# Which operand stands still in the expert value products: coefficients or value rows

## The chip, the cores and the metric

The kernel runs on one core of one Trainium2 chip. The metric is the device time of one execution in microseconds (us). PE is TensorE (PEld its weight loads), DVE is VectorE, ACT is ScalarE, POOL is GpSimd, SP is SyncE, which here only issues DMA.

## The reference, cut to what matters

The program is one attention block with a mixture of experts behind it (`first_block`), and a second block with attention, a state space branch and a gated feed-forward layer (`second_block`), on 256 tokens of 2048 features in fp32. The change touches one sum of the first block, the last line of the expert layer:

```python
idx = jnp.take_along_axis(cand_i, best_j, axis=-1)      # 16 experts of 16384 for each token and head
g = jax.nn.softmax(best_s, axis=-1)
u_sel = jnp.take(u, idx, axis=0)
a = jax.nn.gelu(jnp.einsum('thkd,td->thk', u_sel, hb), approximate=False)
v_sel = jnp.take(v, idx, axis=0)
return jnp.einsum('thk,thkd->td', (g * a).astype(hb.dtype), v_sel)
```

`u` and `v` are 16384 x 2048 tables. The kernel gathers nothing: it computes gelu(u x) for all 16384 experts and 256 tokens, multiplies it by a dense table of the weights g (zero where an expert was not chosen), and multiplies the result, the coefficients, by all of `v`.

## The kernel before, in words

The activations lie as columns: `xT[k]` is a tile of 128 features by 256 tokens, k = 0 to 15. Every fp32 product is made of three matmuls in a faster format: each operand is split into a high and a low part (ACT rounds the high part, DVE subtracts it from the source for the low part), and `mm3` (lines 177 to 182) issues high x high, high x low and low x high into the same PSUM sums. The first argument of `mm3` is the stationary operand (loaded into the array before each matmul, the PEld rows), the second the moving one.

The expert layer works in 128 blocks of 128 experts. For each block `scores` (989) makes 48 matmuls with rows of `u` as the stationary operand and 256 tokens moving, and a gelu. 30 blocks later `coef` (1050) multiplies by the weights and splits the result into `ahi` and `alo` (128 experts x 256 tokens, in the first two blocks a tile named `first`). The value products are cut into 256 half steps: `place(n)` gives the half of the features (1024 of 2048) and the block. Eight blocks of one half follow each other, then the same eight blocks of the other half. For a half step `v_split` (1009) loads two blocks of `v` at a time into a `raw` tile (five such tiles rotate among all loads of the program) and splits 128 experts x 1024 features into `wp` or `vp` tiles, and `v_main` (1085) makes the products: for each 128 of the 1024 features the value rows are the stationary operand and the coefficients of 256 tokens move. That is 8 x 3 = 24 matmuls in a half step. The sums of the first four of the eight feature tiles stay in PSUM (`ps_v`, two banks for a half) through all 128 blocks; those of the other four lie in two `ps_t` banks and are added to `xT` by DVE after each group of eight blocks (`add`, 1109, line 1112).

The order on every engine is the order of the Python code; nothing is rescheduled. The expert loop has three stretches. `FILL` (1141): six half steps alone. The loop (1145): two half steps with 24 score matmuls after each. The end (1157): the remaining half steps without scores, where `v_split` and `ahead` run three steps ahead, and where the parameters of the state space branch and the modulation sums (`self.more`) are worked in. The last half step but one and the last are made together (1174). Behind them comes the norm of the next block: `sq_add` (347) squares each finished `xT` tile on ACT and adds the squares on POOL or DVE, and `make` (394) sums them on PE.

Of the kernel before, what the change touches and what calls it, by code (L numbers as in the profile page):

```python
# [14 lines left out]
OP = mybir.AluOpType  # L15
# [3 lines left out]
KT = D // 128  # L19
T = 256  # L20
# [16 lines left out]
class Pipe:  # L37
# [73 lines left out]
    def add(self, gen):  # L111
        self.side.append(gen)


class Core:
# [11 lines left out]
    def sb(self, pool, name, shape, dt=F32, bufs=1, tag=None):  # L127
        return pool.tile(list(shape), dt, name=name, tag=tag or name, bufs=bufs)
# [337 lines left out]
    def mixer(self, pool, upto):  # L466
        nc, ins, sb = self.nc, self.ins, self.sb
        mm = nc.tensor.matmul
        w_in, w_out = ins["w_in"][0], ins["w_out"][0]
        x, meta = ins["x"][0], ins["meta_tokens"]  # L470
# [16 lines left out]
        rows = [(xa[0], 128), (xa[1], 128), (xm, 16)]  # L487
# [38 lines left out]
            nc.vector.tensor_tensor(self.both, self.ident[:40, 0:8], self.ident[:40, 32:40], op=OP.add)  # L526


        self.xT = [sb(self.glob, "xT", [128, T], bufs=KT) for _ in range(KT)]
        self.gap(self.glob, "hh", 32)  # L530
        hh = sb(self.glob, "hh", [128, KT, N], F32R)
        hl = sb(self.glob, "hl", [128, KT, N], F32R)
# [2 lines left out]
        turned = []  # L535
# [375 lines left out]
    def peer(self, ctx, pool, upto):  # L911
        nc, ins, sb = self.nc, self.ins, self.sb
        mm = nc.tensor.matmul
        u, v = ins["peer_u"][0], ins["peer_v"][0]
        BI, WI = 8, 4
# [48 lines left out]
        turned = []  # L964
# [35 lines left out]
        vt, vs, spare = {}, {}, {}  # L1000
# [4 lines left out]
        def place(n):  # L1005
            b, r = divmod(n, 2 * BI)
            return r // BI, b * BI + r % BI
# [40 lines left out]
        coefs = {}  # L1048

        def coef(i):  # L1050
            if i % WI == 0 and i:
                weights(i // WI + 1)
            a = act.pop(i)
            w = wb[i // WI][:, :, i % WI, :]
            nc.vector.tensor_tensor(a.rearrange("p (c t) -> p c t", c=16), a.rearrange("p (c t) -> p c t", c=16), w, op=OP.mult)  # L1055
            if i < 2:
                hi, lo = (sb(wp, "first", [128, T], F32R, bufs=4) for _ in range(2))
                if i == 1:
                    self.gap(wp, "first", 160)
            else:  # L1060
                if i == 2:
                    self.gap(spare["v"], "ahi", 192)
                hi, lo = (sb(spare["v"], nm, [128, T], F32R, bufs=10) for nm in ("ahi", "alo"))
            nc.scalar.activation(hi, a, AF.Copy)  # L1064
            coefs[i] = (hi, lo)
            return lambda: nc.vector.tensor_tensor(lo, a, hi.bitcast(F32), op=OP.subtract)

        def ahead(n):

            if n < 256:  # L1070
                half, i = place(n)
                if half == 0:
                    return coef(i)
            return nothing
# [5 lines left out]
        with self.tc.tile_pool(name="experts", bufs=1) as ep:  # L1080
            banks = {}
            spare["v"] = ep
            self.gap(ep, "vp", 64)

            def v_main(*ns):


                half, i = place(ns[0])
                end = place(ns[-1])[1]
                if i == 0:  # L1090
                    banks[half] = [self.ps("v") for _ in range(2)]
                if i % BI == 0:
                    banks["t"] = [self.ps("t") for _ in range(2)]

                def at(d):
                    return (banks[half] if d < 4 else banks["t"])[d // 2 % 2][:, (d % 2) * T:(d % 2 + 1) * T]

                for d in range(8):
                    first, last = (i == 0, end == 127) if d < 4 else (i % BI == 0, end % BI == BI - 1)
                    c = slice(d * 128, (d + 1) * 128)  # L1100
                    for n in ns:
                        hi, lo = vs[n]
                        self.mm3(at(d), (hi[:, c], lo[:, c]), coefs[place(n)[1]], first and d % 2 == 0, last and n == ns[-1], skip_group_check=True)
                for n in ns:
                    vs.pop(n)
                    if half == 1:
                        coefs.pop(place(n)[1])

                def add():
                    for d in range(0 if end == 127 else 4, 8):  # L1110
                        x = self.xT[half * 8 + d]
                        nc.vector.tensor_tensor(x, at(d), x, op=OP.add)
                        if end == 127:
                            self.sq_add(half * 8 + d, x)

                return add if end % BI == BI - 1 else nothing

            reorder()
            self.spare = "g"
            n = 0  # L1120

            def half_step(n, block=None, half=0, ticks=0):

                def more(i):
                    if i < ticks:
                        next(self.more, None)

                add = v_main(n)
                low = v_split(n + 1)
                if block:  # L1130
                    block[0](half)
                low()
                more(0)
                if block:
                    block[1](half)
                add()
                low = ahead(n + 2)
                more(1)
                low()

            while n < FILL:
                half_step(n)
                n += 1
            new = blocks(LAG + 1)
            for i in range(LAG, 128):
# [947 lines left out]
```

## Time and profile before

| what | value |
|---|---|
| median of 3 runs (lowest, highest) | 3706.91 us (3699.51, 3732.38) |
| the profiled execution | 3723.51 us |
| its span | 3721.7 us |
| mean granted TensorE clock | 0.99 of full speed |
| PE busy, PEld busy | 98%, 95% of the span |
| DVE, ACT, POOL busy | 76%, 49%, 13% of the span |

The profile is of one execution, and 16.6 us above the median. Matmuls are pipelined and each row lasts until its modelled end, so consecutive rows overlap: how fast PE works is read from the starts of consecutive rows, or from the count of matmuls in a stretch, not from the duration of one row.

### The profile page before, as it was taken

How to read it: one execution, taken by the hardware profiler on the slowest of the kernel's cores; microseconds unless marked ns; L12 is line 12 of the kernel's file. 1: busy time of each engine (PE TensorE's matmuls, PEld its weight loads, DVE VectorE, ACT ScalarE, POOL GpSimd, SP SyncE). 2: the span in 40 equal slices, each digit the busy share in tenths (PEclk: the TensorE clock that was granted, in tenths of full speed). 3: DMA queues.
4: the chain of work that ended last, by engine and by line, in shares of the span. 5: the costliest groups of instructions: out<-in, count | busy, mean ns of one | idle time of the engine just before them, and what ended most of it. 6: DMA issues, size and time to landing. Idle time of an engine off the chain costs nothing.

```text
span 3721.7 us, 72639 instructions
## 1 busy us (share of the span) xinstructions
PE 3629.0 (98%) x30186; PEld 3536.0 (95%) x30186; DVE 2831.7 (76%) x4414; ACT 1819.5 (49%) x2740; POOL 479.7 (13%) x496
## 2 busy tenths in 40 slices
PE   9999999999999999999999999898999999999998
PEld 8989899999899999999999998888889999999998
DVE  5556678988688888888888779999888675656565
ACT  4444444369444444444444456665544554444443
POOL 0000012100000000000000015666520100000000
PEclk9999999999999999999999999999999999999999
DMA  6546464455998999999999756545477675556563
GB/s 207 170 136 204 159 193 151 170 170 201 278 252 245 245 250 254 249 257 251 253 250 255 259 193 200 173 158 175 155 225 240 202 238 190 182 182 196 175 196 125
DMA packets 491481, 768.99 MB, mean 207 GB/s; under 512 B 21050, under 2 KB 332501, under 8 KB 485248
## 3 DMA queue, kind: packets, MB, share of 16 engines
q1 hardware_dynamic: 476160, 712.11, 62.8%
q0 software_dynamic: 14960, 52.23, 5.0%
q8 instruction: 237, 3.88, 0.4%
q14 instruction: 92, 0.75, 0.1%
q10 hardware_dynamic: 32, 0.01, 0.0%
HBM read 734.92 MB, written 27.26 MB: 205 GB/s over the span
## 4 chain that ended last, share of the span: by engine, by line
PE 79%; DVE 10%; ACT 6%; issue 3%; DMA 2%; POOL 0%; SPq 0%; DVEq 0%; POOLq 0%; ACTq 0%
PE ps_g L180 18%; PE ps_g L181 18%; PE ps_g L182 18%; DVE wp L149 4%; PE ps_v L181 3%; PE ps_v L182 3%; PE ps_v L180 3%; PE ps_t L181 3%; PE ps_t L182 3%; PE ps_t L180 3%; DMA raw<-in_peer_u_dram 1%; ACT wp L148 1%; PE ps_t L942 1%; ACT raw L1379 1%; PE ps_v L1377 1%
## 5 line engine op out<-in xcount | busy, mean ns | idle before, releaser
L180 PE MATMUL ps_g<-hh,wp 128*128 128x256 f32 (+1 forms) x5648 | 1608.8, 285 | 0.4 <-ACT wp L148 0.3
L182 PE MATMUL ps_g<-hh,wp 128*128 128x256 f32 (+1 forms) x5648 | 1585.3, 281 | 12.6 <-DVE wp L149 12.6
L181 PE MATMUL ps_g<-hl,wp 128*128 128x256 f32 (+1 forms) x5648 | 1584.1, 280 | 2.8 <-DVE hl L1628 2.8
L149 DVE TENSOR_TENSOR wp<-raw,wp 128x1024 fp32r<-128x1024 f32 (+2 forms) x877 | 1055.3, 1224 | 67.8 <-ACT wp L148 66.8
L180 PEld LDWEIGHTS ps_g<-hh,wp 128*128 128x128 f32 x5648 | 1069.4, 189 | 24.8 <-issue 16.8
L182 PEld LDWEIGHTS ps_g<-hh,wp 128*128 128x128 f32 x5648 | 1070.6, 190 | 16.8 <-DVE wp L149 16.2
L181 PEld LDWEIGHTS ps_g<-hl,wp 128*128 128x128 f32 x5648 | 1072.2, 190 | 3.6 <-DVE hl L1628 3.0
L148 ACT ACTIVATE wp<-raw 128x1024 fp32r<-128x1024 f32 (+2 forms) x877 | 869.8, 1014 | 403.8 <-PE ps_g L181 206.0
L979 DVE STREAM_TRANSPOSE raw<-raw 128x1024 f32<-128x1024 f32 x196 | 242.7, 1239 | 58.0 <-DMA raw<-in_peer_u_dram 56.5
L870 DVE SCALAR_TENSOR_TENSOR macc<-raw,cs,macc 128x512 f32<-128x512 f32 x360 | 283.2, 787 | 3.9 <-DMA raw<-in_w_mod_dram 3.9
L1023 DVE TENSOR_TENSOR wp<-raw,wp 128x1024 fp32r<-128x1024 f32 x155 | 186.5, 1206 | 39.0 <-ACT wp L1021 38.7
L1021 ACT ACTIVATE wp<-raw 128x1024 fp32r<-128x1024 f32 x155 | 163.0, 1055 | 99.2 <-PE ps_t L181 45.0
L180 PE MATMUL ps_g<-act,wp 128*128 128x256 f32 x704 | 199.2, 283 | 0.9 <-ACT act L148 0.9
L181 PE MATMUL ps_g<-act,wp 128*128 128x256 f32 x704 | 198.0, 281 | 0.4
L182 PE MATMUL ps_g<-act,wp 128*128 128x256 f32 x704 | 197.6, 281 | 0.0
L1032 POOL DMA_DIRECT2D wb<-wd x32 | 36.7, 1147 | 1125.3 <-DVE gl L1055 1099.1
L1064 ACT ACTIVATE ahi<-gl 128x256 fp32r<-128x256 f32 x126 | 52.5, 417 | 251.6 <-DVE gl L1055 251.6
L182 PE MATMUL ps_v<-ahi,wp 128*128 128x256 f32 x612 | 169.9, 278 | 0.0
L180 PE MATMUL ps_v<-ahi,wp 128*128 128x256 f32 x612 | 169.9, 278 | 0.0
L181 PE MATMUL ps_v<-alo,wp 128*128 128x256 f32 x612 | 169.6, 277 | 0.0
L180 PE MATMUL ps_t<-ahi,wp 128*128 128x256 f32 x612 | 169.6, 277 | 0.0
L182 PE MATMUL ps_t<-ahi,wp 128*128 128x256 f32 x612 | 169.6, 277 | 0.0
(560 smaller groups left out, 6906.5 us busy)
## 6 DMA issues: line engine op xcount, KB each, us to landing
raw<-in_peer_v_dram SPq DMA_DIRECT2D x128, 1024.0 KB, 8.7
raw<-in_w_in_dram SPq DMA_DIRECT2D x118, 1024.0 KB, 7.3
raw<-in_peer_u_dram SPq DMA_DIRECT2D x392, 256.0 KB, 6.0
raw<-in_w_mod_dram SPq DMA_DIRECT2D x96, 1024.0 KB, 5.4
raw<-in_w_up_dram SPq DMA_DIRECT2D x87, 1024.0 KB, 5.9
raw<-in_w_out_dram SPq DMA_DIRECT2D x32, 1024.0 KB, 5.8
raw<-in_w_down_dram SPq DMA_DIRECT2D x32, 1024.0 KB, 6.9
raw<-in_peer_u_dram SPq DMA_DIRECT2D x30, 1024.0 KB, 5.1
```

The lines of the kernel that those rows point to most:

```text
L148: self.nc.scalar.activation(hi, src, AF.Copy)
L149: self.nc.vector.tensor_tensor(lo, src, hi.bitcast(F32), op=OP.subtract)
L180: mm(out, a[0], b[0], start=start, stop=False, **kw)
L181: mm(out, a[0], b[1], start=False, stop=False, **kw)
L182: mm(out, a[1], b[0], start=False, stop=stop, **kw)
L870: nc.vector.scalar_tensor_tensor(acc, t[:, k], s, acc, op0=OP.mult, op1=OP.add)
L942: nc.tensor.transpose(p[:, k * 128:(k + 1) * 128], t[:, c:c + 128], self.ident)
L979: nc.vector.transpose(out=x, in_=x)
L1021: nc.scalar.activation(hi, src, AF.Copy)
L1023: return lambda: nc.vector.tensor_tensor(lo, src, hi.bitcast(F32), op=OP.subtract)
L1064: nc.scalar.activation(hi, a, AF.Copy)
L1377: mm(p[:, e * 128:(e + 1) * 128], w[:, e], o[:, e], start=True, stop=True)
```

## The change

The operands of the value products change places. The coefficients of 128 tokens become the stationary operand and 512 features of the value rows move, so a half step has 2 chunks of features x 2 halves of the tokens x 3 = 12 matmuls of 512 columns in place of 24 of 256. The sums then lie as rows (tokens on the partitions), not as columns.

For that `xT` is now cut out of four tiles of four k each. The four `xT` tiles of each half that are summed up in groups (k = 4 to 7 and 12 to 15) are turned to rows once, after half steps 1 and 3 (`to_rows`), DVE adds the `ps_t` sums to those rows after each group of eight blocks (`gather`), and at the last block of each half both parts are turned to columns again (`to_columns`): the rows out of `xT`, and the `ps_v` sums by way of a `raw` tile. The order within a half step changes too: the `ps_t` part is made first. A spacing of 192 bytes ahead of `ahi` becomes 64.

```diff
-        self.xT = [sb(self.glob, "xT", [128, T], bufs=KT) for _ in range(KT)]
+        self.x4 = [sb(self.glob, "xT", [128, 4, T], bufs=4) for _ in range(4)]
+        self.xT = [self.x4[k // 4][:, k % 4] for k in range(KT)]
...
-                    self.gap(spare["v"], "ahi", 192)
+                    self.gap(spare["v"], "ahi", 64)
...
+            def rows(half):
+
+                return self.x4[2 * half + 1].rearrange("p a t -> p (a t)").rearrange("p (h d) -> p h d", h=2)
+
+            def to_rows(half):
+
+                for h in range(2):
+                    p = self.ps("g")
+                    for a in range(4):
+                        nc.tensor.transpose(p[:, a * 128:(a + 1) * 128], self.x4[2 * half + 1][:, a, h * 128:(h + 1) * 128], self.ident)
+                    banks["rows", h] = p
+                for h in range(2):
+                    self.copy(rows(half)[:, h], banks.pop(("rows", h)))
+
+            def to_columns(src, tag):
+
+                out = []
+                for j in range(2):
+                    p = self.ps(tag)
+                    for a in range(2):
+                        for h in range(2):
+                            o = (2 * a + h) * 128
+                            nc.tensor.transpose(p[:, o:o + 128], src[:, h, (2 * j + a) * 128:(2 * j + a + 1) * 128], self.ident)
+                    out.append(p)
+                return out
...
-                for d in range(8):
-                    first, last = (i == 0, end == 127) if d < 4 else (i % BI == 0, end % BI == BI - 1)
-                    c = slice(d * 128, (d + 1) * 128)
+                def products(c, h):
+                    first, last = (i % BI == 0, end % BI == BI - 1) if c else (i == 0, end == 127)
                     for n in ns:
-                        hi, lo = vs[n]
-                        self.mm3(at(d), (hi[:, c], lo[:, c]), coefs[place(n)[1]], first and d % 2 == 0, last and n == ns[-1], skip_group_check=True)
...
+                        a, b = coefs[place(n)[1]], vs[n]
+                        t, d = slice(h * 128, (h + 1) * 128), slice(c * 512, (c + 1) * 512)
+                        self.mm3((banks["t"] if c else banks[half])[h], (a[0][:, t], a[1][:, t]), (b[0][:, d], b[1][:, d]),
+                                 first, last and n == ns[-1])
+
+                def gather():
+                    for h in range(2):
+                        nc.vector.tensor_tensor(rows(half)[:, h], rows(half)[:, h], banks["t"][h], op=OP.add)
...
+                products(1, 0)
+                products(1, 1)
+                if end < 127:
+                    products(0, 0)
+                    products(0, 1)
+                    done()
+                    return gather if end % BI == BI - 1 else nothing
+
+                gather()
+                products(0, 0)
+                turned = to_columns(rows(half), "g")
+                products(0, 1)
+                done()
+                flat = lambda q, j: self.x4[q][:, 2 * j:2 * j + 2].rearrange("p a t -> p (a t)")
+                for j, p in enumerate(turned):
+                    self.copy(flat(2 * half + 1, j), p)
+                s = self.raw_tile([128, 2, 512])
+                nc.scalar.copy(s[:, 0], banks[half][0])
+                nc.vector.tensor_copy(s[:, 1], banks[half][1])
+                turned = to_columns(s, "t")
+                for a in range(4):
+                    self.sq_add(8 * half + a, self.x4[2 * half + 1][:, a])
+                for j, p in enumerate(turned):
+                    nc.vector.tensor_tensor(flat(2 * half, j), p, flat(2 * half, j), op=OP.add)
+                    for a in range(2):
+                        self.sq_add(8 * half + 4 + 2 * j + a, self.x4[2 * half][:, 2 * j + a])
+                return nothing
...
             while n < FILL:
                 half_step(n)
+                if n in (1, 3):
+                    to_rows(n // 2)
                 n += 1
```

The order on PE in one half step of the loop, between two rows of scores (`ps_g`). Before, the row of three repeats four times for `ps_v` and four times for `ps_t`:

```order
L182 MATMUL ps_g<-hh,wp 128x256
L180 MATMUL ps_v<-ahi,vp 128x256
L181 MATMUL ps_v<-alo,vp 128x256
L182 MATMUL ps_v<-ahi,vp 128x256
...
L180 MATMUL ps_t<-ahi,vp 128x256
L181 MATMUL ps_t<-alo,vp 128x256
L182 MATMUL ps_t<-ahi,vp 128x256
...
L180 MATMUL ps_g<-hh,wp 128x256
```

Now, with three rows for each of two `ps_t` and two `ps_v` banks:

```order
L182 MATMUL ps_g<-hh,wp 128x256
L180 MATMUL ps_t<-vp,ahi 128x512
L181 MATMUL ps_t<-vp,ahi 128x512
L182 MATMUL ps_t<-vp,alo 128x512
...
L180 MATMUL ps_v<-vp,ahi 128x512
L181 MATMUL ps_v<-vp,ahi 128x512
L182 MATMUL ps_v<-vp,alo 128x512
...
L180 MATMUL ps_g<-hh,wp 128x256
```

The matmuls are half as many and twice as wide; the `ps_t` banks are finished in the middle of the half step instead of at its end.

The order on PE at the last block of the first half (half step 247), where `raw` is the tile that holds the `ps_v` sums:

```order
L182 MATMUL ps_v<-wp,alo 128x512
L1108 MATMUL ps_g<-ident,xT 128x128 x8
L180 MATMUL ps_v<-wp,ahi 128x512
L181 MATMUL ps_v<-wp,ahi 128x512
L182 MATMUL ps_v<-wp,alo 128x512
L1108 MATMUL ps_t<-ident,raw 128x128 x8
L180 MATMUL ps_t<-wp,ahi 128x512
```

Two runs of eight transposes now stand between matmuls; the first waits for DVE's sums (the first row below), the second for the copies of `ps_v`.

The order on DVE at the last step of the second half, before:

```order
L1112 TENSOR_TENSOR xT<-ps_v,xT 128x256 x4
L1112 TENSOR_TENSOR xT<-ps_t,xT 128x256 x3
L370 TENSOR_TENSOR sqx<-sqx 128x256
L1112 TENSOR_TENSOR xT<-ps_t,xT 128x256
L370 TENSOR_TENSOR sqx<-sqx 128x256
```

and now:

```order
L1133 TENSOR_TENSOR xT<-xT,ps_t 128x512 x2
L144 COPY xT<-ps_g 128x512
L1159 COPY raw<-ps_v 128x512
L1164 TENSOR_TENSOR xT<-ps_t,xT 128x512 x2
L370 TENSOR_TENSOR sqx<-sqx 128x256 x2
```

Eight additions of 256 columns have become four additions and two copies of 512 columns, with PE's transposes between the copies and the last additions.

## Rows read from the trace of the kernel before

**Rows 1.** Page, busy us (share of the span) xinstructions; the granted clock by slices.

```profile
PE 3629.0 (98%) x30186; PEld 3536.0 (95%) x30186; DVE 2831.7 (76%) x4414; ACT 1819.5 (49%) x2740; POOL 479.7 (13%) x496
...
PEclk9999999999999999999999999999999999999999
```

**Rows 2.** Windows: start:end length, busy us (x instructions) by engine, clock, DMA share, GB/s.

```profile
1000.00:1197.00 197.00, 197.00 (x1740) 197.00 (x1740) 166.23 (x196) 83.94 (x105) 4.60 (x4) 1.00 0.92 252
1300.00:2050.00 750.00, 750.00 (x6620) 750.00 (x6619) 635.55 (x764) 326.74 (x411) 20.70 (x18) 1.00 0.93 253
2080.00:2206.00 126.00, 126.00 (x1083) 125.83 (x1082) 91.80 (x156) 59.15 (x80) 11.03 (x10) 1.00 0.75 252
```

**Rows 3.** Timeline of PE in a half step of the loop: start, us, instruction.

```profile
1500.58 0.28 PE L180 MATMUL ps_v<-ahi,vp 128*128 128x256 f32 x1
...
1503.30 0.28 PE L180 MATMUL ps_g<-hh,wp 128*128 128x256 f32 x1
```

**Rows 4.** Waits, 1000 to 2000 us: engine line waited for: us, times, longest.

```profile
DVE raw L979 <- DMA raw<-in_peer_u_dram: 46.9, 30, 3.0
...
PEld ps_v L182 <- DVE vp L1023: 1.7, 1, 1.7
```

**Rows 5.** Timeline of PE, 272 moving columns, twelve issues in a row.

```profile
349.71 0.29 PE L182 MATMUL ps_g<-hh,wp 128*128 128x272 f32 x1
...
351.23 0.29 PE L182 MATMUL ps_g<-hh,wp 128*128 128x272 f32 x1
```

**Rows 6.** Windows, 100 us of the feed-forward layer (256 columns).

```profile
3100.00:3200.00 100.00, 100.00 (x851) 100.00 (x850) 56.28 (x75) 42.67 (x52) 0.00 (x0) 1.00 0.61 197
```

**Rows 7.** Timeline of PE, plain fp32 matmuls in a row, and their line: ns min/median/max.

```profile
2266.90 1.13 PE L1846 MATMUL ps_v<-b,b 32*128 32x256 f32 x4
...
L1846 PE MATMUL ps_v<-b,b x128: 374/374/479, 2257.5 to 2652.4; 32*128 32x256 f32 x128
```

**Rows 8.** Timeline of PE, four transposes in a row.

```profile
581.52 0.60 PE L942 MATMUL ps_t<-ident,raw 128*128 128x128 f32 x4
```

**Rows 9.** Groups by shape, 560 to 960 us: xcount | busy us, mean ns | idle before.

```profile
L149 DVE TENSOR_TENSOR wp<-ps_t,wp 128x512 fp32r<-128x512 f32 x118 | 80.0, 684 | 40.9 <-ACT wp L148 40.3
L148 ACT ACTIVATE wp<-ps_t 128x512 fp32r<-128x512 f32 x118 | 69.9, 593 | 74.1 <-PE ps_t L942 73.1
```

**Rows 10.** Timeline of DVE in `FILL`.

```profile
958.40 1.23 DVE L1023 TENSOR_TENSOR vp<-raw,vp 128x1024 fp32r<-128x1024 f32 x1 [0.53 <-ACT vp L1021]
959.55 0.42 DVE L1055 TENSOR_TENSOR gl<-gl,wb 128x256 f32<-128x256 f32 x1
...
961.40 1.23 DVE L1023 TENSOR_TENSOR wp<-raw,wp 128x1024 fp32r<-128x1024 f32 x1 [0.53 <-ACT wp L1021]
...
988.85 1.25 DVE L979 STREAM_TRANSPOSE raw<-raw 128x1024 f32<-128x1024 f32 x1 [5.28 <-DMA raw<-in_peer_u_dram]
```

**Rows 11.** Timeline of PE, the last value matmul and the norm behind it.

```profile
2208.07 0.28 PE L182 MATMUL ps_t<-ahi,wp 128*128 128x256 f32 x1
...
2210.31 1.05 PE L400 MATMUL ps_t<-ones,sqx 128*128 128x1 f32 x8 [0.34 <-DVE sqx L370]
...
2213.78 0.58 PE L180 MATMUL ps_v<-hh,wp 128*128 128x256 f32 x1 [1.18 <-ACT hh L426]
```

**Rows 12.** Timeline of ACT there: squares and a table load.

```profile
2205.57 1.41 ACT L366 ACTIVATE sqx<-xT 128x256 f32<-128x256 f32 x4 [1.38 <-DVE xT L1112]
2207.01 1.28 ACT L361 ACT_TABLE_LOAD   x1
2208.30 1.03 ACT L366 ACTIVATE sqx<-xT 128x256 f32<-128x256 f32 x3
```

More of the change, by code (lines that the diff above doesn't have):

```diff
@@ L1093, in v_main @@
                     banks["t"] = [self.ps("t") for _ in range(2)]
-                def at(d):
-                    return (banks[half] if d < 4 else banks["t"])[d // 2 % 2][:, (d % 2) * T:(d % 2 + 1) * T]
-                for d in range(8):
-                    first, last = (i == 0, end == 127) if d < 4 else (i % BI == 0, end % BI == BI - 1)
-                    c = slice(d * 128, (d + 1) * 128)
-                    for n in ns:
-                        hi, lo = vs[n]
-                        self.mm3(at(d), (hi[:, c], lo[:, c]), coefs[place(n)[1]], first and d % 2 == 0, last and n == ns[-1], skip_group_check=True)
@@ L1104, in v_main @@
[L1104 to L1116, printed above, removed]
+                def products(c, h):
+                    first, last = (i % BI == 0, end % BI == BI - 1) if c else (i == 0, end == 127)
+                    for n in ns:
+                        a, b = coefs[place(n)[1]], vs[n]
+                        t, d = slice(h * 128, (h + 1) * 128), slice(c * 512, (c + 1) * 512)
+                        self.mm3((banks["t"] if c else banks[half])[h], (a[0][:, t], a[1][:, t]), (b[0][:, d], b[1][:, d]),
+                                 first, last and n == ns[-1])
@@ new lines, in gather, with done @@
+                def gather():
+                    for h in range(2):
+                        nc.vector.tensor_tensor(rows(half)[:, h], rows(half)[:, h], banks["t"][h], op=OP.add)
+                def done():
+                    for n in ns:
+                        vs.pop(n)
+                        if half == 1:
+                            coefs.pop(place(n)[1])
+                products(1, 0)
[5 more added lines that the diff above has]
+                    return gather if end % BI == BI - 1 else nothing
```

## The prediction

> **What bounds the kernel.** I read the page first, then windows by stage, the timeline of PE at single issues, the waits, and the timelines at the two places where the change adds work. PE is busy 98% of the span and its clock is granted nearly in full in every slice [rows 1], so the upper of the two levels, 2.4 GHz. The stage of the change is the expert loop and its end, about 955 to 2208 us. In the windows there PE is busy without a break while DVE is busy 84 to 85% in the loop and 73% in the end [rows 2]; in 1000 us the weight loads waited on DVE once, 1.7 us [rows 4]. So PE sets the pace, and what an issue costs is the distance of starts: from the first value matmul of a half step to the first score matmul behind it 2.72 us pass for 24 issues, 113.3 ns each [rows 3]. The window says the same: 6620 matmuls in 750 us are 113.3 ns [rows 2]. 113.3 ns is more than 256 columns at 2.4 GHz need, 106.7 ns. What the extra 6.6 ns are is the question of this change.
>
> **What the swap saves.** All 256 half steps have 24 matmuls before, 6144 in all, and 12 now, 3072; the columns streamed are the same, 1,572,864. Two issues before cost 226.7 ns [rows 3]. No row shows a split-format matmul of 512 columns, so its price is bounded:
> - From below, 512 columns at 2.4 GHz: 213.3 ns, nothing lost. Saving 13.4 ns x 3072 = 41 us.
> - The nearest row of a long issue: four plain fp32 matmuls in a row take 1.13 us from first start to last end; the last lasts 0.374, and the first lasts 0.105 longer than the others, which delays the second; (1.13 - 0.374 - 0.105) / 3 = 217 ns an issue [rows 7]. It holds the array as long as 512 columns do, a weight load of 128 columns is hidden under each, and only some 4 ns are lost. Saving 9.7 x 3072 = 30 us.
> - From above, by column: 272 columns take (351.23 - 349.71) / 12 = 126.7 ns [rows 5], 0.466 ns a column, and 256 columns in the feed-forward layer 100 us / 851 = 117.5 ns [rows 6], 0.459. So 512 could take 235 to 239 ns, a loss of 26 to 37 us.
>
> I take 217 ns. What speaks for it: a transpose streams only 128 columns, and still four of them stand (0.60 - 0.27) / 3 = 110 ns apart [rows 8] (0.27 us is the length of one row). So a change of 128 stationary columns alone costs about 110 ns, whatever moves. At 256 columns this load and the stream (106.7) are of equal length and get in each other's way: 113 ns in the experts, 117.5 in the feed-forward layer, same shape [rows 3, 6]. At 512 columns the load has twice its own time to hide in.
>
> The Trainium skill, "TensorE: Matmul & The Clock Gate", section on the back-to-back issue gap, gives N/2.4 + 2.5 ns for N columns at full clock, so 215.8 ns at 512; by it the saving would be 33 us and the time 3684. The trace does not follow it at 256 columns (109.2 by the rule, 113.3 and 117.5 measured) or at 272 (115.8 against 126.7). If an excess of that size, 4 to 11 ns, belongs to each load, 512 columns take 220 to 227 ns and between 20 us and nothing is saved; this stays in my range.
>
> **What the additions cost.** A transpose is 110 ns on PE, so 8 are 0.9 us [rows 8]. A DVE pass over 128x512 from PSUM is 0.68 us, an ACT pass 0.59 [rows 9].
> - `to_rows`, twice in `FILL`: 0.9 us of PE each. `FILL` does not run at PE's pace: its half step is 3.00 us (958.40 to 961.40) against 2.72 of PE, set by ACT and DVE in turn [rows 10]. The ACT copy now stands ahead of the next `vp` or `wp` part and waits for PE's step and the transposes, so it can delay the next step by up to 3 us. But some 20 us later DVE waits 5.28 us for a DMA of `u` anyway [rows 10], which can swallow it. Between 0 and 6 us in all; I take 3.
> - Group sums: two passes of 0.68 us in place of four of 0.41; DVE is not the bound. The `ps_t` banks are now finished half a step earlier, and 1.3 us of `ps_v` products cover the passes before the next group. Nothing.
> - Last block of the first half: PE waits a little for the sums (0.2), 0.9 for eight transposes, 0.85 for the copy of the second `ps_v` bank (0.68 and the way to it), 0.9 for eight transposes, and 0.5 until DVE has freed the first `ps_t` bank for the next group. 3.3 us. Behind the waiting copies on ACT and DVE stand `v` parts that are needed three steps later, 7.8 us.
> - Last step: again 0.2 + 0.9 ahead of the last products. After the last product the last part of the sum of squares started 2.0 us later before, at 2210.31 against 2208.07 + 0.28 [rows 11]. Now the path is on ACT: copy out of `ps_g` and `ps_v` (1.2, from before the last product ends), five squares of 0.35, the table load of 1.28, four squares [rows 12], which ends about 5.1 us after the last product. The table load was hidden and now is not. Together 1.1 + 3.1 = 4.2 us.
>
> The weight loads still come one with each matmul, loads by DMA and their order are the same, and the new `raw` tile takes one of five places at two moments, when the loads behind it are not needed for 10 us. Sum of additions: 3 + 0 + 3.3 + 4.2 = 10.5 us, with ends of 6 and 17. The smaller spacing of `ahi` only moves addresses; what this does is within the price of the issue.
>
> **The sum.** 3723.5 - 30 + 10.5 = 3704 for the profiled execution. It stood 16.6 us above the median of the three runs, 3706.9; taken from the median the forecast is 3706.9 - 19 = 3688 us, 0.5% faster.
>
> **Rivals.**
> 1. The saving doesn't arrive, because what feeds PE takes over. For: the DMA engines are busy 92 to 93% in the loop [rows 2], and DVE already waited 30 times, 46.9 us in all, for rows of `u` [rows 4]. Against: PE barely noticed (1.7 us), and one block of the loop only shrinks from 96 x 113.3 = 10.88 to 10.64 us, while DMA at 0.93 needs 10.1 and DVE at 0.85 needs 9.2. It decides if the DMA's work per block exceeds 10.64. The loop's share of the saving, 98 blocks x 24 x 9.7 ns = 23 us, would be lost: 3706.9 - 7 + 10.5 = 3710.
> 2. Slower: moving value rows streams no better than the 272-column rows. The weight load and the stream disturb each other over the whole issue, 237 ns by [rows 5, 6]. 10.3 x 3072 = 32 us lost, plus 10.5: 3749. It decides above 226.7 - 10.5/3.072 = 223.3 ns, from where the kernel is slower. Against it: the excess differs between rows of one shape (113.3 and 117.5), so it is not a rate by column.
> 3. The same page and section of the Trainium skill state that a sustained stream of loads and matmuls reaches 131 ns an issue at 512 columns. As a mechanism here: issues would overlap until 512 columns cost 131 ns, 96 x 3072 = 294 us saved, about 3423. The rows speak against it: nothing ever streams faster than 0.443 ns a column [rows 3, 5, 6].
>
> **Chances.** Forecast 0.70 (gains between 0.1 and 0.9%, 3672 to 3703), rival 1 0.20 (3700 to 3717), rival 2 0.08, rival 3 0.02. About 1%, 37 us, is what a measurement of this kernel can tell from no change. The forecast's best end is 41 - 6 = 35 us, so faster by over 1% needs that end and a lucky median, or rival 3: 0.09. Slower by over 1% is the upper part of rival 2: 0.05. The rest, 0.86, lies within 1%. The range: 3670, the best end, to 3716, rival 1's upper end; outside are rival 3 and most of rival 2.
>
> **What would show it.** PE's timeline in a half step: 12 issues about 217 ns apart, and 2.6 us in place of 2.72 to the next score row; wider than 223 ns, and rival 2 holds. The count of matmuls with their columns in 1300 to 2050 says whether PE still works without a break; waits of PE on `vp`, `wp` or `ps_g`'s operands there mean rival 1. At the two ends of a half, idle PE ahead of the transposes of about 1 us, and some 5 us between the last product and the sum of squares. In `FILL`, whether PE's first loop steps come later than before. The forecast is wrong if an issue of 512 columns takes more than 227 ns or well under 213, or if the additions cost more than 17 us.

## The result and the profile after

The changed kernel took 3740.0 us (median of 17 runs, 3735 to 3758), the kernel before 3706.9 in the same batch (17 runs, 3697 to 3743): **1.0076 of before, 95% interval 1.0054 to 1.0098**. It is 0.8% slower, with an interval that does not reach 1, and the time lies outside the range. The profiled execution's span is 3749.0 us, against 3721.7.

From the starts of single matmuls in the two traces:

| stretch | before, us | after, us | difference |
|---|---|---|---|
| ahead of `FILL`, same code | 948.0 | 949.0 | +1.0 |
| `FILL`: first value product to first score of the loop | 23.3 | 24.4 | +1.1 |
| loop: first to last score | 1084.1 | 1104.7 | +20.6 |
| end: last score to last value product | 152.7 | 157.8 | +5.1 |
| last value product to the first product behind the norm | 5.7 | 9.6 | +3.9 |
| from there to the end, same code | 1508.0 | 1503.5 | -4.5 |

The page and the windows come first (length, busy us and instructions by engine, granted clock, DMA share, GB/s):

```profile
PE 3655.6 (98%) x27162; PEld 3422.6 (91%) x27162; DVE 2833.7 (76%) x4352; ACT 1828.0 (49%) x2746; POOL 481.9 (13%) x496
...
PEclk9999999999999999999999999999999999999999
```

```profile
1300.00:2050.00 750.00, 750.00 (x4859) 678.17 (x4858) 618.94 (x713) 321.15 (x404) 19.59 (x17) 1.00 0.91 245
```

PE is busy without a break in the loop, as in [rows 2]; DVE and the DMA engines do a little less per us than before (0.91 against 0.93). In the waits of 1000 to 2000 us (us in all, times, longest) neither PE nor its weight loads have a row any more, and DVE's wait for rows of `u` has shrunk from the 46.9 us of [rows 4]:

```profile
DVE raw L980 <- DMA raw<-in_peer_u_dram: 34.4, 25, 4.1
```

So nothing upstream has taken over: PE itself needs longer. In the loop's 2340 value issues the mean distance of starts is 232.9 ns, where two issues before took 226.7. And the 4704 score matmuls, which the change does not touch, went from 113.35 to 116.0 ns. One block of PE's timeline shows both (start, us, instruction):

```profile
1500.48 0.40 PE L182 MATMUL ps_v<-vp,alo 128*128 128x512 f32 x1
1500.71 0.28 PE L180 MATMUL ps_g<-hh,wp 128*128 128x256 f32 x1
...
1503.45 0.39 PE L180 MATMUL ps_t<-wp,ahi 128*128 128x512 f32 x1
...
1506.01 0.39 PE L182 MATMUL ps_v<-wp,alo 128*128 128x512 f32 x1
1506.24 0.28 PE L180 MATMUL ps_g<-hh,wp 128*128 128x256 f32 x1
...
1509.07 0.39 PE L180 MATMUL ps_t<-vp,ahi 128*128 128x512 f32 x1
```

Twelve value issues take 1506.24 - 1503.45 = 2.79 us, 232.5 ns each; [rows 3] had 2.72 for the same columns. The 24 scores ahead of them take 2.74 us (114 ns), the 24 behind them 2.83 (118 ns): same shape, same line, same tiles, two paces.

The loop's +20.6 us by its parts: the value products cost 2340 x 232.87 - 4680 x 113.37 = 14.3 us more and the scores 4704 x 2.67 = 12.6 more, while PE's waits came to 4.5 us in place of 10.7, 6.2 less.

The end of the last step, on PE, ACT, POOL and DVE, answers to [rows 11, 12]:

```profile
2233.85 1.03 PE L1108 MATMUL ps_g<-ident,xT 128*128 128x128 f32 x8
...
2235.89 0.39 PE L182 MATMUL ps_v<-wp,alo 128*128 128x512 f32 x1
...
2236.34 3.94 POOL L370 TENSOR_TENSOR sqs<-sqs,sqx 128x256 f32<-128x256 f32 x5 [18.05 <-ACT sqx L366]
2237.07 0.75 PEld L1108 LDWEIGHTS ps_t<-ident,raw 128*128 128x128 f32 x7 [0.99 <-DVE raw L1159]
...
2237.54 1.28 ACT L361 ACT_TABLE_LOAD   x1
...
2240.34 1.02 PE L400 MATMUL ps_t<-ones,sqs 128*128 128x1 f32 x4 [2.29 <-POOL sqs L370]
...
2241.22 1.84 PE L400 MATMUL ps_t<-ones,sqx 128*128 128x1 f32 x8
...
2245.49 0.58 PE L180 MATMUL ps_v<-hh,wp 128*128 128x256 f32 x1 [1.19 <-ACT hh L426]
```

The last part of the sum of squares starts 2241.22 - 2236.17 = 5.05 us behind the last product (its start and the 0.28 of [rows 11]); 5.1 was forecast. The path runs over POOL's sums (PE waits 2.29 us for them) as well as over ACT's table load. In `FILL` (DVE):

```profile
958.80 0.68 DVE L144 COPY xT<-ps_g 128x512 f32<-128x512 f32 x1
...
974.14 1.25 DVE L980 STREAM_TRANSPOSE raw<-raw 128x1024 f32<-128x1024 f32 x1 [2.29 <-DMA raw<-in_peer_u_dram]
...
987.66 1.25 DVE L980 STREAM_TRANSPOSE raw<-raw 128x1024 f32<-128x1024 f32 x1 [2.31 <-DMA raw<-in_peer_u_dram]
```

The wait of 5.28 us for `u` in [rows 10] is now 2.31: most of `FILL`'s delay was swallowed there.

### The profile page after: what moved, and what is told of

The parts are those of the page before. It is cut to its first block, busy times and chain, and to the rows that moved or that the text cites. A ratio compares the mean times of both kernels' runs of the same rounds, so it can differ in the third digit from the quotient of the medians.

```text
span 3749.0 us, 66689 instructions
## 1 busy us (share of the span) xinstructions
PE 3655.6 (98%) x27162; PEld 3422.6 (91%) x27162; DVE 2833.7 (76%) x4352; ACT 1828.0 (49%) x2746; POOL 481.9 (13%) x496
## 4 chain that ended last, share of the span: by engine, by line
PE 80%; DVE 10%; ACT 6%; issue 2%; DMA 1%; POOL 0%; POOLq 0%; DVEq 0%; ACTq 0%
PE ps_g L180 18%; PE ps_g L182 18%; PE ps_g L181 18%; DVE wp L149 4%; PE ps_v L181 4%; PE ps_v L182 4%; PE ps_v L180 4%; PE ps_t L182 3%; PE ps_t L180 3%; PE ps_t L181 3%; ACT wp L148 1%; PE ps_t L943 1%; ACT raw L1432 1%; PE ps_v L1430 1%; DMA raw<-in_peer_v_dram 1%
## 5 line engine op out<-in xcount | busy, mean ns | idle before, releaser
L999 ACT ACTIVATE gl<-ps_g 128x256 f32<-128x256 f32 x128 | 49.1, 383 | 285.7 <-PE ps_g L182 285.4
L1024 DVE TENSOR_TENSOR vp<-raw,vp 128x1024 fp32r<-128x1024 f32 x101 | 122.3, 1211 | 75.5 <-ACT vp L1022 75.3
L2019 DVE SCALAR_TENSOR_TENSOR cv<-ps_g,cols_b,cv 128x255 f32<-128x255 f32 x84 | 40.6, 483 | 160.0 <-ACT cv L2018 159.9
L2018 ACT ACTIVATE cv<-ps_g,cols_b 128x256 f32<-128x256 f32 x84 | 47.7, 568 | 219.1 <-PE ps_g L182 219.1
L181 PEld LDWEIGHTS ps_g<-act,wp 128*128 128x128 f32 x704 | 134.0, 190 | 1.1 <-DVE act L149 1.1
```

The source lines that it names most:

```text
L181: mm(out, a[0], b[1], start=False, stop=False, **kw)
L999: nc.scalar.activation(a, p[:, :T], AF.Gelu)
L1024: return lambda: nc.vector.tensor_tensor(lo, src, hi.bitcast(F32), op=OP.subtract)
L2018: nc.scalar.activation(t, p[:, :T], AF.Identity, scale=w[2], bias=self.conv_b[:, f:f + 1])
```

## The experiments

Two theories for the value issue. **STREAM**, later **FORMAT**: rows of split fp32 enter PE at 0.443 ns a column at best (113.3 ns for 256), so 512 cannot take less than 226.7. **COLLISION**: 512 would take 217, but the load of the next 128 stationary columns disturbs the stream. For the scores the theories are **ADDRESS** (it matters where the tiles lie), and at last **PHASE** (the way in which a run of issues is entered sets its pace, which the run then keeps) against **CROWDING** (other work beside the scores slows them). A few more names are told in the expectations that use them. Issue distances are means in the loop (medians, marked m, where waits of PE or a change of format mix in); times are medians.

| run | time, us | of before (95%) | value, ns | score, ns | loop, us | end, us |
|---|---|---|---|---|---|---|
| before | 3706.9 | | 113.4 | 113.4 | 1084.1 | 152.7 |
| change | 3740.0 | 1.0076 (1.0054 to 1.0098) | 232.9 | 116.0 | 1104.7 | 157.8 |
| e1 two of 256 | 3740.4 | 1.0047 (1.0007 to 1.0087) | 117.6 | 114.4 | 1103.2 | 155.8 |
| e2 load 32 | 3736.2 | 1.0051 (1.0016 to 1.0086) | 232.0 | 113.8 | 1094.7 | 156.6 |
| e3 spacing 192 | 3728.4 | 1.0022 (0.9988 to 1.0057) | 229.2 | 114.5 | 1093.0 | 155.7 |
| e4 no turns | 3735.9 | 1.0054 (1.0024 to 1.0084) | 232.9 | 116.1 | 1107.1 | 153.5 |
| e5 before, load 32 | 3703.6 | 0.9965 (0.9927 to 1.0003) | 113.4 | 113.4 | 1081.5 | 149.1 |
| e6 bf16 | 3704.0, one run | | 216 m | 118 m | 1079.8 | 147.2 |
| e7 width 384 | 3666.4, one run | | 173 m | 118 m | 1070.4 | 128.8 |
| e8 hi twice | 3740.8 | 1.0054 (1.0022 to 1.0086) | 232.8 | 116.0 | 1108.2 | 157.8 |
| e9 before, bf16 | 3689.8 | 0.9927 (0.9885 to 0.9968) | 109 m | 113 m | 1081.5 | 143.7 |
| e10 bf16, 192 | 3706.5 | 0.9956 (0.9922 to 0.9990) | 216 m | 118 m | 1081.1 | 147.2 |
| e11 spacing 128 | 3746.2, one run | | 231.3 | 115.7 | 1104.0 | 157.5 |
| e12 spacing 320 | 3738.3, one run | | 232.9 | 116.1 | 1107.4 | 157.8 |
| e13 last narrow | 3734.4, one run | | 232.8 | 114.0 | 1096.6 | 157.5 |
| e14 score narrow | 3736.0, one run | | 232.4 | 114.4 | 1097.2 | 157.8 |
| e15 before, reset | 3710.6 | 1.0021 (0.9979 to 1.0063) | 113.4 | 113.4 | 1087.5 | 150.2 |
| e16 bf16, reset | 3685.3 | 0.9923 (0.9895 to 0.9952) | 109 m | 113 m | 1076.9 | 143.7 |
| e17 before, resets | 3704.8 | 0.9944 (0.9913 to 0.9975) | 113.5 | 113.5 | 1086.6 | 152.7 |

### Width and load

**e1**: the swapped operands, but two issues of 256 columns in place of one of 512.

```diff
-self.mm3(bank[h], (a[0][:, t], a[1][:, t]), (b[0][:, d], b[1][:, d]), first, ...)
+for q in range(2):
+    d = slice(c * 512 + q * 256, c * 512 + (q + 1) * 256)
+    self.mm3(bank[h][:, q * 256:(q + 1) * 256], (a[0][:, t], a[1][:, t]), (b[0][:, d], b[1][:, d]), first and q == 0, ...)
```

> The changed kernel, but each value product of 512 columns is issued as two of 256 with the same stationary coefficients: 24 matmuls in a half step again, operands still swapped. Theory STREAM (moving columns cost 0.443 ns each at best, 113.3 ns for 256, so two of 256 cost what one of 512 does; the rest is a disturbance by the weight load that depends on addresses): the issues take 113 to 118 ns; if the width of 512 is what disturbs, they and the scores lie at 113.3 and the time is about 3740 - 14 - 13 = 3713 us; if the swapped addresses are, they stay near 116 to 118 and the time stays near 3740. Theory COLLISION (an issue of 512 columns would take 216 ns, and what lies above comes from its weight load): halving the width doubles the loads, so the time is not below 3740.

```profile
1486.58 0.28 PE L180 MATMUL ps_t<-vp,ahi 128*128 128x256 f32 x1
...
1489.41 0.29 PE L180 MATMUL ps_g<-hh,wp 128*128 128x256 f32 x1
```

24 issues in 2.83 us, 117.9 ns, and the time of the change: halving the width again gives nothing back. So the swap had put the value products into the slower pace, near 118 ns for 256 columns, and the width then gained 2 x 117.6 - 232.9 = 2.3 ns an issue.

**e2, e5**: 32 stationary columns in place of 128 in the value products (but for the first of a group), in the changed kernel and in the one before.

```diff
+w = 128 if first else 32
-t = slice(h * 128, (h + 1) * 128)
+t = slice(h * 128, h * 128 + w)
...
```

> The changed kernel, but only the first block of each group loads 128 stationary columns; all others load 32 (the products of 96 of 128 tokens are left out). The moving columns stay 512. A load of 32 columns takes about a quarter of the time. STREAM: an issue falls from 232.9 to about 227 ns and not below, 3072 x 5.9 ns = 18 us, and scores perhaps back to 113.3: 3709 to 3722 us. COLLISION: without most of the load an issue falls to about 217 ns, 49 us: about 3691 us or, with the scores, 3678.

> The kernel before, but only the first block of each group loads 128 stationary columns of value rows; all others load 32 (the products of 96 of 128 features are left out). Moving columns stay 256. STREAM: the issue stays at 113.3 ns, since 256 columns take that long: 3707 us, no change. COLLISION (or a bound by the load): 109 ns, 6144 x 4.3 ns = 26 us: about 3681 us.

e2, then e5:

```profile
1481.93 0.40 PE L180 MATMUL ps_t<-vp,ahi 128*32 128x512 f32 x1
...
1484.72 0.28 PE L180 MATMUL ps_g<-hh,wp 128*128 128x256 f32 x1
```

```profile
1465.45 0.28 PE L180 MATMUL ps_v<-ahi,vp 128*32 128x256 f32 x1
...
1468.17 0.28 PE L180 MATMUL ps_g<-hh,wp 128*128 128x256 f32 x1
```

With loads of 32 columns, 512 moving columns still take 2.79 / 12 = 232.5 ns and 256 still 2.72 / 24 = 113.3: the load does not make the floor, and COLLISION falls. STREAM's forecast for e2, 227, failed too: the 6 ns above the floor do not go with the load either. The pace near 118 did go: the scores of e2 fell to 113.8, and in the end of e5 the value issue fell from 115.9 to 113.4. (e5 alone would not show this: e15, with the code of before in its end, took 114.0 there.) That the load has a part in that pace is what e13 and e14 test.

**e4**: the turns to rows and columns left out.

```diff
-turned = to_columns(rows(half), "g")
...
-if n in (1, 3):
-    to_rows(n // 2)
```

> The changed kernel without the transposes and copies that turn columns to rows and back (the sums are added untransposed, which leaves the turning out). Both theories: the issues of 512 columns stay near 233 ns and the scores near 116; the time falls by what the turning costs, by the traces 1.0 in the first half steps, about 1 at the end of the first half and 3 to 4 before the norm: 4 to 6 us, 3734 to 3736 us. My prediction had put this at 10.5 us: 3730.

Against the change the traces give `FILL` 24.4 to 23.4, the end 157.8 to 153.5, the norm 9.6 to 5.4: the additions cost 9.5 us. `FILL`'s 1.0 is known to about 1 us only, since the code of the change takes 24.2 to 25.8 us there in the other traces. The medians of the times differ by 4 us, within their scatter.

### Format and width

**e6, e9**: the coefficients and value rows as bf16 pairs, with 512 columns in the changed kernel and 256 in the one before. (Such a pair holds fewer bits of a number.)

```diff
-hi, lo = (self.sb(self.glob, "wp", [128, 1024], F32R, bufs=NWP) for _ in range(2))
+hi, lo = (self.sb(self.glob, "wp", [128, 2048], BF16, bufs=NWP)[:, :1024] for _ in range(2))
...
```

> The changed kernel with the coefficients and the value rows held as bf16 pairs in place of split fp32 pairs: the same 512 columns and the same number of issues in the value products, 2-byte operands. FORMAT (the floor of 226.7 ns is the rate at which 4-byte rows enter, 0.443 ns a column): the value issue falls to 213 to 218 ns, the loop by about 35 us from 1104.7. ISSUE (what is lost belongs to each issue, or to the two engines' reads, whatever the format): it stays at 227 to 234 ns. The scores stay in the old format and should keep 113 to 118 ns.

> The kernel before, with its coefficients and value rows held as bf16 pairs; 256 columns an issue as before. FORMAT (4-byte rows enter at 0.443 ns a column at best; 2-byte rows at 2.4 GHz and 2.6 ns an issue, as in the run with 512 bf16 columns): the value issue falls from 113.4 to about 109 ns, 6144 x 4 = 25 us less, loop at 1070 at the least, where DVE and DMA took over in the run with 384 columns: 3685 to 3697 us. LOAD (as the prediction read it: at 256 columns the load of 128 stationary columns and the stream are of equal length and disturb each other, so that 113.4 stays): no change, 3707 to 3711.

e6, eight issues, then e9, 22 issues:

```profile
1477.76 0.38 PE L180 MATMUL ps_t<-vp,ahi 128*128 128x512 bf16 x1
...
1479.49 0.38 PE L182 MATMUL ps_v<-vp,alo 128*128 128x512 bf16 x1
```

```profile
1462.14 0.27 PE L181 MATMUL ps_v<-alo,wp 128*128 128x256 bf16 x1
...
1464.54 0.27 PE L182 MATMUL ps_t<-ahi,wp 128*128 128x256 bf16 x1
```

1.73 / 8 = 216 ns and 2.40 / 22 = 109.1: under 3 ns an issue over 213.3 and 106.7, at either width. These two runs alone leave the load as a rival, for the weight loads of bf16 are shorter too. Loads of the change, of e2 and of e6 (ns min/median/max):

```profile
L180 PEld LDWEIGHTS ps_t<-wp,ahi x306: 186/188/192, 958.1 to 2231.5; 128*128 128x128 f32 x153
L180 PEld LDWEIGHTS ps_v<-wp,ahi x306: 107/108/112, 958.9 to 2223.4; 128*32 128x32 f32 x153
L180 PEld LDWEIGHTS <-ahi x1008: 95/98/181, 958.2 to 2199.2; 128*128 128x128 bf16 x168
```

e2 and e5 had loads of 108 ns, nearly as short as the 98 of bf16, and stayed at 232 and 113.3. So the 113.3 of [rows 3] is a property of the 4-byte format, and FORMAT holds. e6 is also the change at the price that I had forecast, and its loop gained only 4 us on before: the value issues gained 25 us, but the scores went to 118 and lost about 20.

**e7**: 384 of each 512 value columns.

```diff
+w = 512 if first else 384
-d = slice(c * 512, (c + 1) * 512)
+d = slice(c * 512, c * 512 + w)
...
```

> The changed kernel with each value product cut from 512 to 384 columns (a quarter of the value features is left out of the sums, apart from the first product of each group). FORMAT: time goes by the column, 384 x 0.443 = 170 ns at best and, with the excess of 2.7% seen at 512 columns, 175 ns. ISSUE: 384 columns at 2.4 GHz are 160 ns and the 19.5 ns that an issue of 512 lost stay, 180 ns.

Issues (start, us), a window as above, and waits (us in all, times, longest) in 1300 to 2050:

```profile
1473.57 0.34 PE L180 MATMUL ps_t<-wp,ahi 128*128 128x384 f32 x1
...
1475.65 0.28 PE L180 MATMUL ps_g<-hh,wp 128*128 128x256 f32 x1
```

```profile
1300.00:2050.00 750.00, 707.45 (x5019) 691.23 (x5018) 633.16 (x729) 331.41 (x415) 22.45 (x21) 0.99 0.96 255
```

```profile
DVE raw L980 <- DMA raw<-in_peer_u_dram: 56.0, 29, 3.9
...
PE ps_t L180 <- DVE xT L1134: 29.0, 16, 2.9
```

2.08 / 12 = 173.3 ns, 0.451 a column: it goes by the column, and ISSUE's 180 falls. Here what feeds PE sets the pace, as rival 1 had it: PE is idle for 43 of 750 us, the DMA share is 0.96, and the loop stops at 1070 us, 14 below before. Of PE's waits the longest, 29 us, is for the group sums, which I had costed at nothing. Whether DVE or the DMA engines make this floor was not tested.

### What the addresses do

**e3, e11, e12, e10**: the spacing ahead of the coefficients at 192, 128 and 320 bytes; e10 is 192 with bf16 pairs. **e8**: the same moving tile in two issues that follow each other (its edit is shortened below).

```diff
-self.gap(spare["v"], "ahi", 64)
+self.gap(spare["v"], "ahi", 192)
```

```diff
-mm(a[0], b[0]); mm(a[0], b[1]); mm(a[1], b[0])
+mm(a[0], b[0]); mm(a[1], b[0]); mm(a[0], b[1])
```

> The changed kernel with the spacing ahead of the coefficients put back from 64 to 192 bytes, nothing else. ADDRESS (the excess of the value issue over 226.7 ns, and of the scores over 113.4, comes from where the stationary and the moving tiles lie to each other): the value issue moves by more than 2 ns in one direction, and the scores by more than 1 ns, the loop by 5 us or more from 1104.7. If the addresses play no part: 233 and 116 ns, and the loop stays within 2 us.

> The changed kernel with a spacing of 128 bytes ahead of the coefficients. ADDRESS: another pair of values for the value issue and the scores than 232.9 and 116.0 (spacing 64) or 229.2 and 114.5 (spacing 192), between 226.7 and 236 and between 113.3 and 118. It is open which.

> The changed kernel with a spacing of 320 bytes ahead of the coefficients, 256 more than in the change. ADDRESS with a period of 256 bytes or a part of it: the same 232.9 and 116.0 as with 64. With a longer period: other values.

> The changed kernel with bf16 pairs and the spacing ahead of the coefficients at 192. ADDRESS: the scores fall from 117.7 to below 116 ns, the loop from 1079.8 to about 1070, at which upstream takes over; 3694 us. Without a part of the addresses: as with bf16 pairs alone, 1080 and 3704.

> The changed kernel with the three products of a split pair issued as hi x hi, lo x hi, hi x lo, so that the moving tile is the same in two issues that follow each other and changes in two of three (before: hi, lo, hi). ALTERNATION (the part over 226.7 ns is paid when the moving tile changes): two issues of three at 234, one at 227, mean 231.5, and the issue behind the repeated tile is the short one. If the change of tile plays no part: 233 as before, without a pattern by line.

e3:

```profile
1477.22 0.39 PE L180 MATMUL ps_t<-wp,ahi 128*128 128x512 f32 x1
...
1479.96 0.28 PE L180 MATMUL ps_g<-hh,wp 128*128 128x256 f32 x1
```

2.74 / 12 = 228.3 ns. The value issue is 232.9, 231.3, 229.2 and 232.9 ns at 64, 128, 192 and 320 bytes: 320 repeats 64, as a period of 256 would, which one repeat suggests and does not prove. Of the distances between value issues in the loop none is under 225 ns, at any spacing; at 192 the first of each three takes 226.5 on average, and at 64 each of the three takes 232 or more. So the floor of 226.7 is seen at 512 columns too, and what moves with the spacing lies above it. With the spacing of before, the change costs 11.7 us less in the loop and its time can't be told from no change. ALTERNATION fell (the three lines take 232.3, 232.6 and 234.0 on average, as in the change). In bf16 the spacing did nothing (e10: loop 1081.1 against 1079.8), so ADDRESS as put there failed. How an address comes to cost these nanoseconds stays open.

### How a run of scores gets its pace

In the trace of the change the distance from the last value issue to the first score tells the pace of all 24 scores, in the 182 half steps whose coefficients are `ahi` and `alo` and whose scores follow straight on. It is 229 or 230 ns in 91 of them, and the scores' median distance is 118 in every one; it is 233 to 236 in the other 91, and the median is 113 in every one. The fence of the block above shows one of each: 1500.48 to 1500.71 (235 ns unrounded), 1506.01 to 1506.24 (230).

**e13, e14**: one issue of each half step with 32 stationary columns: the last value product, or the second score (both edits are shortened below).

```diff
-mm(o, a[1][:, t], b[0][:, d], start=False, ...)
+mm(o[:32], a[1][:, h * 128:h * 128 + 32], b[0][:, d], start=False, ...)
```

```diff
-mm(o, a[0], b[1], start=False, ...)
+mm(o[:32], a[0][:, :32], b[1], start=False, ...)
```

> The changed kernel in which one issue of each half step, the last value product ahead of the scores, has 32 stationary columns in place of 128 (96 of its 128 rows are left out of that one product); all others as in the change. In the trace of the change the distance from that issue to the first score goes with the pace of all 24 scores behind it: 229 to 230 ns and they run at 118, 235 to 236 ns and they run at 113. PHASE (the pace of the run is set by how it is entered and then holds itself): the edit of one issue moves all scores of the runs behind it, to 113.3 if a short load puts the pair right; the scores' mean then falls from 116.0 to about 113.5, and the loop by 8 to 12 us. CROWDING (the scores are slow for what works beside them, and the distance ahead is only another sign of it): 116 as before.

> The changed kernel in which the second of the 24 score issues of each half step has 32 stationary columns in place of 128 (the rest of that product is left out). PHASE: the 22 behind it run at 113.3 in every half step, mean 113.5 in place of 116.0, loop 8 to 12 us shorter. CROWDING: only the issue with the short load changes, mean 116.

e13, then e14:

```profile
1483.11 0.40 PE L1131 MATMUL ps_v<-wp,alo 128*32 128x512 f32 x1
1483.34 0.28 PE L180 MATMUL ps_g<-hh,wp 128*128 128x256 f32 x1
...
1486.07 0.39 PE L1129 MATMUL ps_t<-vp,ahi 128*128 128x512 f32 x1
```

```profile
1482.10 0.28 PE L999 MATMUL ps_g<-hl,wp 128*32 128x256 f32 x1
...
1484.50 0.28 PE L181 MATMUL ps_g<-hl,wp 128*128 128x256 f32 x1
1484.61 0.28 PE L182 MATMUL ps_g<-hh,wp 128*128 128x256 f32 x1
```

All 182 runs of scores of that kind now go at 113, in e13 and in e14. One short load sets the pace of the 22 or 24 issues behind it, and the loop falls by 8.1 and 7.5 us. CROWDING falls. PHASE holds with an exception: behind the coefficients of the first two blocks, the tiles named `first`, two runs of e13 and one of two in e14 stay at 118 with the short load in place. One of e13's:

```profile
991.14 0.39 PE L1131 MATMUL ps_v<-wp,first 128*32 128x512 f32 x1
991.37 0.28 PE L180 MATMUL ps_g<-hh,wp 128*128 128x256 f32 x1
...
994.20 0.40 PE L1129 MATMUL ps_t<-vp,first 128*128 128x512 f32 x1
```

24 scores take 2.83 us, 118 ns each. The 12 runs of e13 that have eight other matmuls between the short load and the scores go at 118 too. So a short load does not set the pace everywhere, and what it does inside PE is not shown.

**e15, e16**: in the kernel before (e16: with bf16 pairs), four issues more, one in each down projection of the feed-forward layer, into a half bank that nothing reads. Such an issue with a short load is called a reset here.

```diff
+if reset and f == 1 and k == 0:
+    self.nc.tensor.matmul(p[:32, n:2 * n], parts(k)[0][:, :32], xs(k)[0], start=False, stop=False, ...)
```

> The kernel before with four issues more: in each of the four down projections of the feed-forward layer, behind the first product of the second chain, one matmul of 256 columns with 32 stationary columns into a half of the bank that nothing reads. In the trace of before the 1726, 1527 and 1437 issues behind the first waits of these projections run at 117.8 ns to the last, where 618 and 414 issues of the same shape just before run at 113.3. PHASE: the one short load puts the pair right and the pace of 113.3 holds to the next wait: some 5600 issues x 4.4 ns = 25 us less and 0.5 for the four issues, 3685 us. CROWDING: nothing changes, 3708 to 3712.

> The kernel before with bf16 pairs in the value products (0.9927 of before) and the same four issues more. If both act by themselves: 0.9927 less 25 us, 3665 us, 0.986 of before. If the reset does nothing: 3690.

e15:

```profile
3098.66 0.28 PE L181 MATMUL ps_g<-act,wp 128*128 128x256 f32 x1
3098.78 0.28 PE L182 MATMUL ps_g<-act,wp 128*128 128x256 f32 x1
3098.90 0.28 PE L224 MATMUL ps_g<-act,wp 128*32 128x256 f32 x1
3099.01 0.28 PE L180 MATMUL ps_g<-act,wp 128*128 128x256 f32 x1
```

```profile
3100.00:3200.00 100.00, 100.00 (x885) 100.00 (x884) 57.68 (x78) 44.40 (x55) 0.00 (x0) 1.00 0.64 206
```

885 matmuls in the window of [rows 6], which had 851: 113 ns in place of 117.5. The pace then holds for 1722 issues, to the next wait. From the first down projection to the end the trace has 607 us; before had 627. Yet the median did not move, against the expectation. The traces of all runs show why in part: the same code without a reset takes 607, 613, 620 or 627 us there, by how many of its three long stretches happen to be entered at either pace. Of the 16 traces without resets, the one of before is the only one with all three at 118; six have none, and the mean is 613 us. So resets there could be expected to gain some 5 us, not the 25 that I took from that one trace. And before's own times crowd near 3700 and near 3740 (3695 to 3753 in all), and those of e15 do so too: six runs of ten from 3695 to 3712, four from 3733 to 3741. The four resets do not touch what splits them. e16 came to 0.9923 and not 0.986, no better than e9 by more than the scatter.

**e17**: the reset also in every fourth block of the loop.

```diff
+if i >= LAG and i % 4 == 0 and k == 0:
+    nc.tensor.matmul(p[:32, T:2 * T], at(k)[0][:, :32], part(k)[0], start=False, stop=False, ...)
```

> The kernel before with short loads that set the pace, split fp32 kept: the four in the down projections as in the run before, and one in every fourth block of the expert loop (25 issues of 256 columns with 32 stationary columns, 2.8 us in all), into a half of the bank that nothing reads. Nothing is left out. CHANCE (the pace of whole stages in before is set by how a wait happens to end, the loop's too, and so its time differs from run to run, 3695 to 3753): the runs of this kernel above 3720 go, of which before had 7 of 23 and the kernel with four short loads 4 of 10; the kernel with narrow value loads, where every half step sets the pace, had none of 10. All runs 3685 to 3715, median near 3700, 0.25% under before. If the spread has another cause: runs above 3720 in a third of the cases, as before, median 3710.

All 12 runs lie between 3699.0 and 3711.5; of the 17 runs of before in that batch nine were above 3730, and of e15's ten, with the same resets in the down projections, four. So the resets in the loop removed the upper group. That this group is the expert loop at the other pace is inferred: the size fits, 9384 issues x 4.4 ns = 41 us, but no trace of before caught its loop at 118, and in e17's own trace the loop takes 1086.6 us, no less than before's 1084.1.

**A version that beats both**: e16, 3685.3 us, 0.9923 of before, as much as the bf16 pairs give by themselves (e9, 0.9927); without the coarser pairs, e17, 0.9944. What e17 gains is the upper group: the six fastest runs of before in that batch, 3698 to 3709, are as fast as its own.

## Why the prediction was wrong

- **What bounds the kernel** was right: PE sets the pace before and after.
- **The price of 512 columns is the step that failed.** I took 217 ns from [rows 7], which is plain fp32 with 32 rows and 256 columns, and explained the 6.6 ns over 106.7 as a load as long as the stream [rows 8]. The rows of the right format were [rows 3, 5]: 0.443 and 0.466 ns a column, 227 to 239 ns, so that 227 was the gain's end and not its middle. I set them aside because rows of one shape differ (113.3 and 117.5). They differ by pace, not by shape: e15 turned the one into the other. Measured: 226.7 at the floor, and 232.9 with this spacing, which is over the 227 that the prediction named as the sign of being wrong; +14.3 us in the loop and about +1 in the end, where -30 stood for all value products.
- **The skill's rule.** The Trainium skill, "TensorE: Matmul & The Clock Gate", section on the back-to-back issue gap, gives N/2.4 + 2.5 ns, which it calls the gap of a single isolated matmul, 215.8 at 512. The bf16 runs agree (216 and 109.1); for split fp32 the traces do not (232.9 and 113.3). Its 131 ns for a sustained stream, rival 3, shows in no run: the least is 216.
- **What I left out** is nearly as large: untouched matmuls pay for how they are entered, +12.6 us on the scores. I had priced only instructions that the diff touches. The spacing, which I passed over as part of the price, made 11.7 us of the loop's 20.6 (values and scores together).
- **The additions** were right in sum: 9.5 us (e4) for 10.5, made of `FILL` 1.0 for 3 and the rest 8.5 for 7.5, so two misses partly cancel. The last part of the sum of squares came 5.05 us behind the last product, for 5.1, although the forecast did not have POOL's sums in that path.
- **Rival 1** did not decide at 233 ns. But the loop did not go under 1070 us even in e7, and 217 ns would have given 4704 x 113.35 + 2340 x 217 + 10 = 1051. By that estimate the forecast would have lost 19 us there even at its own price.
- **Rival 2** came nearest, and its threshold of 223.3 ns held. Its mechanism did not: loads make neither the 226.7 (e2, e5) nor, in e2, the 6 ns above it.
- **The base.** I treated 16.6 us between the profiled execution and the median as scatter. The profile had all three stretches of the down projections at 118 ns, [rows 6] among them, which is 20 us over the fastest traces of the same code. That is enough for the 16.6; no trace of an execution at the median was kept.

## What to carry to other kernels

Price an issue from rows of the same data format, by the column, before reading its excess as an overhead that a wider issue saves. Compare equal matmuls in different places of a trace: if they run at two paces, ask what stands ahead of each run, and count on an edit to change it for neighbours it does not touch. When the same code takes different times from run to run, compare traces stage by stage before trusting a median of a few runs.

## What the runs showed of the hardware

- At a granted clock of 1.00 in the loop, issues of split fp32 take 113.3 ns at best for 256 columns, and 229 to 233 on average for 512, with single distances from 225; of bf16 they take 109 and 216.
- Equal matmuls of 256 split columns hold either 113.3 or near 118 ns for up to 1726 issues. Which one is settled where the run is entered, behind a wait or another issue. One load of 32 columns in place of 128, in the issue just ahead of the run or in its second, put the run at 113.3 in all 182 cases of e13 and of e14 with `ahi`, and not in three with `first`.
- Moving the coefficients by 128 bytes changed the 512-column issue from 232.9 to 229.2 ns.
